# Where the stationary halves start: 64 or 192 bytes into their buffers

## The chip, the core and the metric

The kernel runs on one core of a Trainium2 chip. A core has a matrix engine (TensorE, PE in the profile, with its weight loads shown apart as PEld), a vector engine (VectorE, DVE), a scalar engine (ScalarE, ACT), GpSimd (POOL) and a queue engine (SyncE, SP) that here issues most of the transfers from the chip's memory. Data lie in an on-chip memory of 128 partitions (SBUF); a product is accumulated in a second memory (PSUM). The metric is the device time of one execution in microseconds, lower is better. The kernel before takes 1235.01 us, the median of three runs (1234.71 to 1235.12).

## The reference

A decoder trunk of two layers works on 256 tokens of width 2048, in float32. Cut to what matters:

```python
def reference(x, c, ada_w, ada_b, ln_g, ln_b, a_in_w, ..., a_out_w, kv_w, b_in_w, b_out_w):
    for layer in range(2):
        shift, scale, gate = _adaln(c, ada_w[layer], ada_b[layer])
        h = x * (1.0 + scale) + shift
        if layer < 1:
            y = _ssd_mixer(h, a_in_w[i], ..., a_out_w[i])      # h @ in_w (10304 wide), conv, scan, gate, @ out_w
        else:
            y = _dilated_mixer(h, k_sh, v_sh, b_in_w[i], b_out_w[i])   # h @ in_w (4096 wide), attention, gate, @ out_w
        x = _layer_norm(ALPHA * x + (1.0 + gate) * y, ln_g[layer], ln_b[layer])
        if layer == 0:
            k_sh, v_sh = _shared_kv(x, kv_w)                    # x @ kv_w (6144 wide)
    return x
```

Nearly all the work is in the products of 256 rows of activations with big weight matrices.

## The kernel before

**Each factor is split in two.** A weight piece of 128 partitions by 1024 columns (512 KB) is loaded into `raw` (`load_piece`, L90), ScalarE copies it, rounded, into `whi` (`split`, L100), and VectorE writes what the rounding left out into `wlo` (L102). The activations have been split likewise. A product is then high by high, high by low and low by high, in a rounded float32 type (fp32r) in which TensorE goes over its moving columns once. `raw` has six buffers, `whi` and `wlo` four each. A buffer of `whi` or `wlo` has 1088 columns, 4352 bytes in a partition, though a half needs 1024 columns; `halves_at(off)` takes the 1024 columns that begin `off` columns into the buffer. The pair `off` is given by one of two names: `SHORT` is 16 columns (64 bytes) for both halves, `LONG` is 0. In the built program the four `whi` buffers start at bytes 53504, 57856, 62208 and 66560 of a partition, those of `wlo` at 70912, 75264, 79616 and 83968, and the activations at 88320: all of these are multiples of 256.

**There are three ways to multiply.** In each, TensorE first loads 128 by 128 stationary values (LDWEIGHTS) and then streams moving columns past them (MATMUL).

- A *token-major* product (`tm_mults`, L213 to L215) holds activations in TensorE and streams 512 columns of `whi` or `wlo`, which lie at offset 0 (`LONG`). At the end of the kernel a few of these stream 256 columns.
- A *quad* (`cm_piece`, L151 to L153) holds 128 columns of `whi` or `wlo` (offset 64 bytes, `SHORT`) and streams 256 columns of the high or of the low activations: three matmuls for each 128 columns of weights and each 128 rows of the contraction.
- A *wide product* (`cm_wide`, L182 and L185) also holds weights, but streams the high and the low activations together: for each of 16 steps along the contraction, two matmuls of 512 columns with two blocks of `whi` (L182), then two of 256 columns with two blocks of `wlo` (L185). Its weights use `SHORT` too.

There are 40 wide products: 12 that make the mixer's inputs (`xs_wide`), 12 for the keys, and in the last layer 12 for the queries and four for the gate (`queries`, `z_gate`). That is 640 steps of four matmuls.

**The order is that of the code, with one piece begun ahead.** The list `upcoming` names the first piece of the next product and the offset it is to be written at; `begin_next` splits that piece while the last piece of the product before is multiplied, so that the next product finds its first halves in `ready`. `firsts` fills this list for the mixer, two more lines for the keys and the queries. The offset there and the one in `cm_wide` belong together. Behind the products, `background` takes small jobs from a list: the dot products of the modulation (L295), each with a transfer of 1 MB that SP issues, the steps of the normalization, and others.

Of the kernel before, what the change touches and what calls it, by code (L numbers as in the profile page):

```python
# [27 lines left out]
NG = 3  # L28
# [21 lines left out]
def trunk(ctx, tc, xT, x, c, par, cst, bias, lnrow, ada, wdt, win, wxs, wout, wk, wv, wbin, wbout, out):  # L50
# [28 lines left out]
    tri = cc[:, CT:CT + 128]  # L79
    ones = cc[:, CM:CM + 128]  # L80
    cons.tile([P, 32], F32, name="pad")
    SHORT, LONG = (16, 16), (0, 0)

    def rows(t, b):

# [2 lines left out]
    def load_piece(src):  # L88
        raw = wp.tile([P, 1024], F32, name="raw", bufs=6)
        nc.sync.dma_start(raw, src)  # L90
        return raw
# [5 lines left out]
    def split(raw, into=None, after=None, off=(0, 0)):  # L97

        hi, lo = into or halves_at(off)
        copied.append(S.activation(hi, raw, AF.Copy))  # L100
        with tc.issue_after(after) if after is not None else ExitStack():
            latest.append(V.tensor_tensor(lo, raw, hi.bitcast(F32), op=ALU.subtract))  # L102
        return hi.rearrange("p (k n) -> p k n", k=2), lo.rearrange("p (k n) -> p k n", k=2)

    jobs, latest, copied, pin = [], [], [], [None]
    upcoming, ready, owed = [], [], []

    def settle():

        while owed:  # L110
            with tc.issue_after(copied[-1].ins), tc.issue_after(latest[-1].ins):
                owed.pop(0)()

    def first_or(src, q, off=(0, 0)):

        return ready.pop() if ready else split(load_piece(src[q]), off=off)

    def begin_next():

        if upcoming:  # L120
            src, q, off = upcoming.pop(0)
            ready.append(split(load_piece(src[q]), off=off))

    def behind_next():

        stack = ExitStack()
        if ready:
            stack.enter_context(tc.issue_after(copied[-1].ins))
            stack.enter_context(tc.issue_after(latest[-1].ins))
        return stack  # L130

    def background(n, every=1):

        state[0] += n
        while state[0] >= every and jobs:
            state[0] -= every
            jobs.pop(0)()
# [17 lines left out]
    def acc_pair(pool=None):  # L155
        return [(pool or mm).tile([P, 2, L], F32, name="acc") for _ in range(2)]
# [11 lines left out]
    def cm_wide(src, dst, rate=(0, 1), moving=None, later=False):  # L168

        both, high = moving or (lambda kt: xp[:, kt], lambda kt: xhi[:, kt, :])  # L170
        ps = acc_pair()
        for q in range(KT // 4):
            w = first_or(src, q, SHORT)
            if q == 1:
                settle()
            if q == KT // 4 - 1:
                begin_next()
            hi, lo = (t.rearrange("p k n -> p (k n)").rearrange("p (k n) -> p k n", k=4) for t in w)
            for k in range(4):
                kt = 4 * q + k  # L180
                for n in range(2):
                    T.matmul(ps[n], hi[:, k, n * P:n * P + P], both(kt), start=kt == 0, stop=False,  # L182
                             skip_group_check=True)
                for n in range(2):
                    T.matmul(ps[n][:, 0, :], lo[:, k, n * P:n * P + P], high(kt), start=False, stop=kt == KT - 1,  # L185
                             skip_group_check=True)
            background(*rate)
        def put():
            for n in range(2):
                S.activation(dst[:, n, :], ps[n][:, 1, :], AF.Copy)  # L190
                V.tensor_tensor(dst[:, n, :], ps[n][:, 0, :], dst[:, n, :], op=ALU.add)

        if later:
            owed.append(put)
        else:
            with behind_next():
                put()
# [20 lines left out]
    def tm_pair():  # L218
        return [mm.tile([P, 512], F32, name="acc") for _ in range(2)]
# [103 lines left out]
    def drain():  # L323
        while jobs:
            jobs.pop(0)()
# [8 lines left out]
    with ExitStack() as cA:  # L334
# [15 lines left out]
        with ExitStack() as cS:  # L350
# [437 lines left out]

            def firsts(kind, g):
                if kind == "xs" and g > 1:  # L790
                    return [(wxs[2 * g - 4 + w], 0, SHORT) for w in range(2)]
                src, k0, _ = begun.get((kind, g), (None, 0, None))
                if src is None:
                    src = win[{"bc": g // 2, "xs": 4 + g, "z": 6 + g}[kind]]
                return [(src, k0 // 2, LONG if kind == "z" else SHORT)]
# [176 lines left out]
    def evict_v(hq, g, ps):  # L972
        vt[hq, g] = place(3 * hq + g if hq == 0 else 9 + g, [P, 2, 512])
        with behind_next():
            for b in range(2):
                S.activation(vt[hq, g][:, b, :], ps[b], AF.Copy)

    with ExitStack() as cL:
        pl = cL.enter_context(tc.tile_pool(name="pl", bufs=3))

        vps = [tm_pair(), tm_pair()]
        def high(i, b):
            for k in range(2):
                kt = 2 * (i // 2) + k
                for w in first_v[i]:
                    T.matmul(vps[i % 2][b], hx(kt)[:, b * P:b * P + P], w[:, k, :], start=kt == 0 and w is first_v[i][0],  # L986
                             stop=False)

        def low(i, b):
            for k in range(2):  # L990
                T.matmul(vps[i % 2][b], lx(2 * (i // 2) + k)[:, b * P:b * P + P], first_v[i][0][:, k, :], start=False,
                         stop=False)

        end, _ = x_quad(0)
        with tc.issue_after(end.ins):
            for n in range(1, 4):
                normalise(0, 512 * n, 512 * n + 512)
        for i in range(4):
            high(i, 0)
        for i in range(4):  # L1000
            if i == 2:
                _, tile4 = x_quad(1)
                for n in range(1, 4):
                    normalise(1, 512 * n, 512 * n + 512)
            low(i, 0)
        for i in range(4):
            high(i, 1)
            if i == 2:
                x_tile(4)
                x_tile(5)  # L1010
        for i in range(4):
            low(i, 1)
        for q in range(2, KT // 2):
            if q < KT // 2 - 1:
                x_tile(2 * q + 2)
                x_tile(2 * q + 3)
            for j in range(2):
                with tc.issue_after(end.ins):
                    w = split(load_piece(wv[2 * j][q]), after=tile4.ins if q == 2 else None)
                tm_mults(q, w, vps[j], hx, lx, 0, KT, range(2))  # L1020
        for g in range(2):
            evict_v(0, g, vps[g])

        R = (1, 2)
        pin[0] = latest[-1].ins
        with tc.issue_after(tile4.ins):
            state[0] = 0
            queue(pl, cols1[11:])
            jobs.append(lambda: gate_out(1))
            upcoming.extend((wk[2 * (2 * g + hq) + w], 0, SHORT) for hq in range(2) for g in range(NG) for w in range(2))  # L1030
            upcoming.extend((wv[1 + 2 * g], 0, LONG) for g in range(NG))
            evict_v(0, 2, tm_chunk(wv[4], hx, lx, rate=R))
            for hq in range(2):
                for g in range(NG):
                    kv[hq, g] = place(3 + 3 * hq + g, [P, 4, L])
                    for w in range(2):
                        cm_wide(wk[2 * (2 * g + hq) + w], kv[hq, g][:, 2 * w:2 * w + 2, :], rate=R, later=True)
            for g in range(NG):
                evict_v(1, g, tm_chunk(wv[1 + 2 * g], hx, lx, rate=R))
            drain()  # L1040
            late = latest[-1].ins

        ada_bias(1, slice(0, KT), slice(0, 2))
        for kt in range(KT):
            t = pl.tile([P, L], F32, name="htmp")
            S.activation(t, xhi[:, kt, :].bitcast(F32), AF.Identity, bias=shift(1, kt), scale=scale(1, kt))
            V.scalar_tensor_tensor(t, xlo[:, kt, :].bitcast(F32), scale(1, kt), t, op0=ALU.mult, op1=ALU.add)
            split_act(xhi[:, kt, :], xlo[:, kt, :], t)
# [29 lines left out]

    def queries(hq):
        qq = [pc2.tile([P, 4, L], F32, name=f"q{g}") for g in range(NG)]  # L1080
        upcoming.extend([(wbin[2 * (2 * g + hq) + w], 0, SHORT) for g in range(NG) for w in range(2)][1:])
        for g in range(NG):
            for w in range(2):
                cm_wide(wbin[2 * (2 * g + hq) + w], qq[g][:, 2 * w:2 * w + 2, :], rate=(1, 1),
                        later=(g, w) != (NG - 1, 1))
        return qq
# [291 lines left out]
```

## Time and profile before

| | |
|---|---|
| median of the runs | 1235.01 us (1234.71 to 1235.12) |
| the profiled execution, first to last instruction | 1233.4 us |
| TensorE busy | 1219.2 us, 99% |
| weight loads | 1048.7 us, 85% |
| VectorE busy | 1027.8 us, 83% |
| ScalarE busy | 701.2 us, 57% |
| moved from and to memory | 335.92 MB, 272 GB/s |
| granted TensorE clock | 1.000 |

The profiled execution's span is 1.6 us under the median of the runs, which also hold what lies before its first and after its last instruction. A row of the groups gives the engine, the operation, what it writes and reads, the shapes, the count, and then the busy time and the mean of one. For a matmul the mean of one runs from its start to its modelled end, and the next begins long before that; what a matmul costs in a row of many is the distance from its start to the next one's.

### The profile page before, as it was taken

How to read it: one execution, taken by the hardware profiler on the slowest of the kernel's cores; microseconds unless marked ns; L12 is line 12 of the kernel's file. 1: busy time of each engine (PE TensorE's matmuls, PEld its weight loads, DVE VectorE, ACT ScalarE, POOL GpSimd, SP SyncE). 2: the span in 40 equal slices, each digit the busy share in tenths (PEclk: the TensorE clock that was granted, in tenths of full speed). 3: DMA queues.
4: the chain of work that ended last, by engine and by line, in shares of the span. 5: the costliest groups of instructions: out<-in, count | busy, mean ns of one | idle time of the engine just before them, and what ended most of it. 6: DMA issues, size and time to landing. Idle time of an engine off the chain costs nothing.

```text
span 1233.4 us, 18854 instructions
## 1 busy us (share of the span) xinstructions
PE 1219.2 (99%) x7132; PEld 1048.7 (85%) x7132; DVE 1027.8 (83%) x1464; ACT 701.2 (57%) x1048; POOL 3.9 (0%) x8
## 2 busy tenths in 40 slices
PE   8999999999999999999999999999999999999998
PEld 7889988898888888888888788888888888888886
DVE  6999986999988989899768678888978866758776
ACT  4554477878597789764335544434445644445551
POOL 0000000000000000000000000000000000000001
PEclk9999999999999999999999999999999999999999
DMA  9999977687656556698998569989998774464673
GB/s 377 423 420 422 421 255 248 224 299 252 215 199 209 168 171 205 217 338 345 362 316 293 196 202 372 347 344 371 382 384 306 232 256 144 122 199 128 206 257 69
DMA packets 81371, 335.92 MB, mean 272 GB/s; under 512 B 9200, under 2 KB 9984, under 8 KB 68480
## 3 DMA queue, kind: packets, MB, share of 16 engines
q1 hardware_dynamic: 80352, 333.33, 75.0%
q0 software_dynamic: 576, 1.05, 0.6%
q8 instruction: 56, 0.92, 0.3%
q10 hardware_dynamic: 352, 0.34, 0.1%
q14 instruction: 35, 0.29, 0.1%
HBM read 331.45 MB, written 3.23 MB: 271 GB/s over the span
## 4 chain that ended last, share of the span: by engine, by line
PE 81%; DMA 10%; DVE 6%; ACT 2%; issue 1%; DVEq 0%; ACTq 0%; SPq 0%
PE acc L182 24%; PE acc L185 12%; PE acc L214 11%; PE acc L215 11%; PE acc L213 11%; DMA raw<-in_win 5%; DMA araw<-in_ada 3%; DVE wlo L102 2%; DVE araw L295 2%; PE py L776 1%; ACT whi L100 1%; PE acc L151 1%; PE acc L153 1%; PE acc L152 1%; PE acc L986 1%
## 5 line engine op out<-in xcount | busy, mean ns | idle before, releaser
L100 ACT ACTIVATE whi<-raw 128x1024 fp32r<-128x1024 f32 x389 | 408.5, 1058 | 358.7 <-PE acc L215 128.9
L102 DVE TENSOR_TENSOR wlo<-raw,whi 128x1024 fp32r<-128x1024 f32 x389 | 469.2, 1220 | 147.8 <-ACT whi L100 139.1
L182 PE MATMUL acc<-actT,whi 128*128 128x512 f32 x1280 | 402.7, 394 | 0.0
L185 PEld LDWEIGHTS acc<-actT,wlo 128*128 128x128 f32 x1280 | 239.6, 188 | 53.5 <-DVE wlo L102 0.5
L214 PE MATMUL acc<-wlo,actT 128*128 128x512 f32 x656 | 257.4, 392 | 2.8 <-DVE wlo L102 2.8
L185 PE MATMUL acc<-actT,wlo 128*128 128x256 f32 x1280 | 253.8, 280 | 0.0
L213 PE MATMUL acc<-whi,actT 128*128 128x512 f32 x656 | 253.5, 394 | 0.0
L295 DVE SCALAR_TENSOR_TENSOR araw<-araw,cb__72 128x2048 f32<-128x2048 f32 x95 | 217.0, 2284 | 2.9 <-DMA araw<-in_ada 2.6
L182 PEld LDWEIGHTS acc<-actT,whi 128*128 128x128 f32 x1280 | 193.9, 188 | 0.4
L215 PE MATMUL acc<-whi,actT 128*128 128x512 f32 x432 | 168.8, 391 | 0.0
L214 PEld LDWEIGHTS acc<-wlo,actT 128*128 128x128 f32 x656 | 123.2, 188 | 30.3 <-DVE wlo L102 5.1
L213 PEld LDWEIGHTS acc<-whi,actT 128*128 128x128 f32 x656 | 122.6, 188 | 24.2
L151 PE MATMUL acc<-actT,whi 128*128 128x256 f32 x372 | 103.1, 281 | 1.5 <-ACT actT L502 0.9
L153 PE MATMUL acc<-actT,wlo 128*128 128x256 f32 x372 | 101.9, 282 | 1.3 <-DVE wlo L102 1.1
L152 PE MATMUL acc<-actT,whi 128*128 128x256 f32 x372 | 103.1, 280 | 0.0
L215 PEld LDWEIGHTS acc<-whi,actT 128*128 128x128 f32 x432 | 81.1, 188 | 16.5
L215 PE MATMUL acc<-whi,ylo 128*128 128x512 f32 x224 | 87.6, 391 | 0.0
L151 PEld LDWEIGHTS acc<-actT,whi 128*128 128x128 f32 x372 | 69.6, 188 | 2.8 <-ACT actT L502 1.3
L153 PEld LDWEIGHTS acc<-actT,wlo 128*128 128x128 f32 x372 | 68.9, 188 | 2.5 <-DVE wlo L102 2.3
L152 PEld LDWEIGHTS acc<-actT,whi 128*128 128x128 f32 x372 | 70.6, 190 | 0.2
L215 PEld LDWEIGHTS acc<-whi,ylo 128*128 128x128 f32 x224 | 42.1, 188 | 8.5
L734 ACT ACTIVATE seg<-cbc,cumT 128x128 f32<-128x128 f32 x128 | 41.1, 389 | 3.5 <-PE py L776 2.1
(311 smaller groups left out, 1151.8 us busy)
## 6 DMA issues: line engine op xcount, KB each, us to landing
araw<-in_ada SPq DMA_DIRECT2D x96, 1024.0 KB, 7.2
raw<-in_win SPq DMA_DIRECT2D x109, 512.0 KB, 6.5
raw<-in_wout SPq DMA_DIRECT2D x64, 512.0 KB, 5.6
raw<-in_wbin SPq DMA_DIRECT2D x64, 512.0 KB, 3.8
raw<-in_wxs SPq DMA_DIRECT2D x48, 512.0 KB, 4.4
raw<-in_wv SPq DMA_DIRECT2D x48, 512.0 KB, 7.2
raw<-in_wk SPq DMA_DIRECT2D x48, 512.0 KB, 7.8
cbc<-cumd SPq DMA_DIRECT2D x16, 512.0 KB, 5.4
```

What stands on the lines that cost most here:

```text
L100: copied.append(S.activation(hi, raw, AF.Copy))
L102: latest.append(V.tensor_tensor(lo, raw, hi.bitcast(F32), op=ALU.subtract))
L151: T.matmul(o, hi[:, k, c_], ahi[:, kt, :], start=first, stop=False, skip_group_check=True)
L152: T.matmul(o, hi[:, k, c_], alo[:, kt, :], start=False, stop=False, skip_group_check=True)
L153: T.matmul(o, lo[:, k, c_], ahi[:, kt, :], start=False, stop=kt == k1 - 1, skip_group_check=True)
L182: T.matmul(ps[n], hi[:, k, n * P:n * P + P], both(kt), start=kt == 0, stop=False, skip_group_check=True)
L185: T.matmul(ps[n][:, 0, :], lo[:, k, n * P:n * P + P], high(kt), start=False, stop=kt == KT - 1, skip_group_check=True)
L213: T.matmul(o, h_, hi[:, k, :], start=kt == k0, stop=False, skip_group_check=part)
L214: T.matmul(o, h_, lo[:, k, :], start=False, stop=False, skip_group_check=part)
L215: end = T.matmul(o, l_, hi[:, k, :], start=False, stop=kt == k1 - 1, skip_group_check=part)
L295: return V.scalar_tensor_tensor(raw, raw, 1.0, cb_, op0=ALU.mult, op1=ALU.mult, accum_out=mod[layer][:, ct, j:j + 1])
L734: S.activation(seg[:, hh, b, :], cbc[:, hh, b, :], AF.Relu, bias=cumT[:, b, h0 + hh:h0 + hh + 1], scale=-1.0)
```

## The change

A third name, `WIDE`, 48 columns (192 bytes) for both halves, takes the place of `SHORT` wherever a piece is split for a wide product: in `cm_wide` itself and in the three lists that begin the first piece of a wide product ahead. The quads keep 64 bytes, the token-major products 0. Shapes, counts, buffers and the order of the instructions on every engine stay as they are; a half then takes bytes 192 to 4288 of its 4352. What differs is the address that ScalarE and VectorE write, and that the weight loads of the wide products read.

```diff
@@ -79,7 +79,7 @@
-    SHORT, LONG = (16, 16), (0, 0)
+    SHORT, WIDE, LONG = (16, 16), (48, 48), (0, 0)
@@ -170,7 +170,7 @@
         both, high = moving or (lambda kt: xp[:, kt], lambda kt: xhi[:, kt, :])
         ps = acc_pair()
         for q in range(KT // 4):
-            w = first_or(src, q, SHORT)
+            w = first_or(src, q, WIDE)
             if q == 1:
                 settle()
@@ -788,7 +788,7 @@
             def firsts(kind, g):
                 if kind == "xs" and g > 1:
-                    return [(wxs[2 * g - 4 + w], 0, SHORT) for w in range(2)]
+                    return [(wxs[2 * g - 4 + w], 0, WIDE) for w in range(2)]
@@ -1027,7 +1027,7 @@
-            upcoming.extend((wk[2 * (2 * g + hq) + w], 0, SHORT) for hq in range(2) for g in range(NG) for w in range(2))
+            upcoming.extend((wk[2 * (2 * g + hq) + w], 0, WIDE) for hq in range(2) for g in range(NG) for w in range(2))
@@ -1078,7 +1078,7 @@
-        upcoming.extend([(wbin[2 * (2 * g + hq) + w], 0, SHORT) for g in range(NG) for w in range(2)][1:])
+        upcoming.extend([(wbin[2 * (2 * g + hq) + w], 0, WIDE) for g in range(NG) for w in range(2)][1:])
```

## The prediction

> **What bounds the kernel now.** I read the page's busy times and its chain of waits first, to see which engine sets the end.
>
> ```profile
> PE 1219.2 (99%) x7132; PEld 1048.7 (85%) x7132; DVE 1027.8 (83%) x1464; ACT 701.2 (57%) x1048; POOL 3.9 (0%) x8
> PE 81%; DMA 10%; DVE 6%; ACT 2%; issue 1%; DVEq 0%; ACTq 0%; SPq 0%
> PE acc L182 24%; PE acc L185 12%; PE acc L214 11%; PE acc L215 11%; PE acc L213 11%; DMA raw<-in_win 5%; DMA araw<-in_ada 3%; DVE wlo L102 2%; DVE araw L295 2%; PE py L776 1%; ACT whi L100 1%; PE acc L151 1%; PE acc L153 1%; PE acc L152 1%; PE acc L986 1%
> ```
>
> TensorE is the chain: 81% of it, and the two lines of the wide products alone (L182, L185) are 36% of the span, some 444 us. A busy matrix engine may still be streaming slower than it could, so next come the groups by shape, for the counts, and then the chain in order of time inside the wide products, for what one step costs.
>
> ```profile
> L182 PE MATMUL acc<-actT,whi 128*128 128x512 f32 x1280 | 402.7, 394 | 0.0
> L185 PE MATMUL acc<-actT,wlo 128*128 128x256 f32 x1280 | 253.8, 280 | 0.0
> L182 PEld LDWEIGHTS acc<-actT,whi 128*128 128x128 f32 x1280 | 193.9, 188 | 0.4
> L185 PEld LDWEIGHTS acc<-actT,wlo 128*128 128x128 f32 x1280 | 239.6, 188 | 53.5 <-DVE wlo L102 0.5
> ```
>
> ```profile
> 256.92 0.46 PE acc L182 x2
> ...
> 278.41 0.46 PE acc L182 x2
> ```
>
> 1280 matmuls of each kind in fours make 640 steps. Each chain row above begins one step; between these two lie 31 steps in 21.49 us, so one step takes 0.6932 us, and in the sequence of the key products the rows are spaced the same. Nothing is waited for: the idle time before both MATMUL groups is 0.0.
>
> **What a matmul costs elsewhere.** The change moves only addresses, so the question is whether the address of the stationary values changes a matmul's price. The timeline shows loads and matmuls together, here in a quad (start, duration, engine):
>
> ```profile
> 211.14 0.28 PE L152 MATMUL acc<-actT,whi 128*128 128x256 f32 x1
> 211.15 0.19 PEld L153 LDWEIGHTS acc<-actT,wlo 128*128 128x128 f32 x1
> 211.26 0.28 PE L153 MATMUL acc<-actT,wlo 128*128 128x256 f32 x1
> ```
>
> The load for the next matmul starts with the matmul before it and runs beside it: two streams read the on-chip memory at once. Four pairs of timeline rows then price the same fp32r matmul in four places.
>
> ```profile
> 211.73 0.28 PE L151 MATMUL acc<-actT,whi 128*128 128x256 f32 x1
> ...
> 214.09 0.28 PE L153 MATMUL acc<-actT,wlo 128*128 128x256 f32 x1
> ```
>
> ```profile
> 250.07 0.28 PE L152 MATMUL acc<-actT,whi 128*128 128x256 f32 x1
> ...
> 251.54 0.28 PE L153 MATMUL acc<-actT,wlo 128*128 128x256 f32 x1
> ```
>
> ```profile
> 1219.58 0.28 PE L213 MATMUL acc<-whi,s 128*128 128x256 f32 x1
> ...
> 1220.90 0.28 PE L215 MATMUL acc<-whi,s 128*128 128x256 f32 x1
> ```
>
> ```profile
> 639.83 0.39 PE L213 MATMUL acc<-whi,actT 128*128 128x512 f32 x1
> ...
> 642.33 0.39 PE L215 MATMUL acc<-whi,ylo 128*128 128x512 f32 x1
> ```
>
> A quad's 256 columns (weights at 64 bytes) cost 2.36 us over 20 distances, 0.118, in the first pair, and 1.47 over 13, 0.113, in the second: same code, same addresses, two prices. At the end of the kernel 256 columns with the stationary values at offset 0 cost 1.32 over 11, 0.120. 512 columns with offset 0 cost 2.50 over 11, 0.227. Now the wide step: two of 512 and two of 256. With the dear price, 2 x 0.227 + 2 x 0.120 = 0.694, which is what it takes (0.693). With the cheap one, 2 x 0.227 + 2 x 0.113 = 0.680. So **the wide step pays today, at 64 bytes, the price that the rows show for offset 0**; the quads pay less at the same 64 bytes, and in some stretches nothing extra. No transfer and no other engine sets these prices, since the rows between each pair are spaced alike whatever runs beside them; what is left is how the load's reads fall against the moving reads.
>
> **The change part by part.** The split itself: ScalarE and VectorE write the halves 128 bytes further on.
>
> ```profile
> L100 ACT ACTIVATE whi<-raw x40: 1061/1062/1067, 580.8 to 685.6; 128x1024 fp32r<-128x1024 f32 x40
> L100 ACT ACTIVATE whi<-raw x47: 1048/1065/1069, 767.0 to 894.5; 128x1024 fp32r<-128x1024 f32 x47
> ```
>
> The first row is a stretch of token-major products (offset 0), the second the key products (offset 64): the medians are 1062 and 1065 ns, so the writer does not care, and I cost this part at nothing. If it did, by even 50 ns a piece, the cover would be the wait below: ScalarE stands idle for TensorE there.
>
> The wide step: no row has weights at 192 bytes, so I bound it. Below: the cheapest prices shown, 0.680, a saving of 0.0124 us if I take the unrounded distances (0.6932 against 2 x 0.2273 + 2 x 0.1131 = 0.6808); times 640 steps that is 7.9 us. Above: the dearest that the rows show for a wide step, which is in the first steps of the key products:
>
> ```profile
> 766.48 0.47 PE acc L182 x2
> 767.18 0.47 PE acc L182 x2
> 767.89 0.46 PE acc L182 x2
> 768.58 0.46 PE acc L182 x2
> ```
>
> 0.70, then 0.71, then 0.69: two steps in 1.41 us, 0.705 each, are 0.0118 us more than the settled 0.6932, which over 640 steps would be 7.6 us. I take the lower bound. My reason is that the wide step already sits at the dear end of every settled row: there is one dearer price, and it lasts two steps, while the cheap one holds for hundreds of matmuls in the quads once it is reached. A new phase between the two streams has more room to gain than to lose. From the 7.9 us I take 0.4 for the four products that run among the attention's small matmuls (some 8 of 16 steps each have other work between, 4 x 8 x 0.0124), since there the phase is broken each time. **Sum: -7.5 us**, 1233.4 to 1225.9 in the profiled execution, and with the 1.6 us that lie outside its span, **1227.5 us** for the median of the runs.
>
> Would the saved time reach the end? These rows are the waits and the stretches of the keys (766 to 899) and of one mixer pair:
>
> ```profile
> ACT s L190 <- PE acc L185: 34.3, 9, 4.6
> ACT whi L100 <- DMA raw<-in_wk: 10.4, 4, 3.4
> ```
>
> ```profile
> 285.00:307.30 22.30, 22.30 (x135) 19.43 (x130) 22.30 (x41) 22.14 (x43) 0.00 (x0) 1.00 0.76 266
> 766.30:899.40 133.10, 133.10 (x769) 116.73 (x768) 114.55 (x119) 56.96 (x74) 0.00 (x0) 1.00 0.94 363
> ```
>
> Among the keys ScalarE waits 34.3 us for TensorE and 10.4 for transfers, which fill 0.94 of their time there at 363 GB/s. A step 1.8% shorter asks for 370 GB/s, and the page shows slices of over 420, so they follow, without much to spare. In the mixer pair VectorE is busy 22.30 of 22.30 us; if it sets the pace there instead, the 12 mixer products (12 x 16 x 0.0124 = 2.4 us) give nothing, which the range holds.
>
> **The rivals.** *Nothing changes* (1235.0). The price follows a pattern that repeats every 64 or 128 bytes, and 192 falls on the same place as 64. For it: the wide prices are the same in all four buffers of the ring, which lie 256 bytes apart within each 1024. Against it: 64 and 0 have different rows, 0.118 and 0.120, so 64 is not a full period of the pattern; 128 may be. A rule bears on this: the Trainium skill, "SBUF — State Buffer", section "Who interferes with whom", says that TensorE has two independent read ports, one for the moving operand and one for LDWEIGHTS, and that "PE and ACT never wait on anyone"; by it the address could not matter at all and the time would be 1235.0. The pair 0.118 and 0.113 for the same quad speaks against taking it that far.
>
> *It gets slower* (1242.6). The step settles at the transient price of 0.705 instead of 0.6932: 640 x 0.0118 = 7.6 us. The place is L182 to L185 in all 640 steps; the mechanism is that a stationary row 128 bytes further on makes its reads meet the moving reads in the matmuls of 512 columns as well, which today, by their 0.227 in the token-major rows, lose nothing extra. It decides as soon as the extra for the two long matmuls exceeds the 0.0124 us that the two short ones can give back. For it: such steps exist. Against it: they give way to the settled step after two.
>
> *Half of it* (1231.2): one of the two short matmuls becomes cheap, 640 x 0.0062 = 4.0 us. I count it with the faster case. *The change doesn't do what it says*: a first piece begun ahead keeps 64 bytes; then 40 of 160 pieces would be unchanged. The three lists are changed along with the product, so I give this nothing.
>
> **How the numbers follow.** Faster 0.47 (the full sum likelier than half), unchanged 0.33, slower 0.20. A measurement of this kernel tells about 0.2%, 2.5 us, from no change, and all the priced cases lie beyond that or at zero, so the three chances are these. The predicted time is that of the likeliest, 1227.5. Its own range is 1226 to 1232.5. The range reaches from 1225.5 (the whole 7.9 us, and 1.6 more for an error of 0.0025 us in the distance of a step as read from rows of two decimals) over the unchanged case to 1239.0, a slower case of half the transient's price; left out is the full slower case and what lies beyond.
>
> **What would show it.** Right: the chain rows of L182 in the wide products stand 0.680 or 0.681 us apart instead of 0.693, the quads and token-major rows keep their distances, and ScalarE's 34.3 us of waiting for TensorE among the keys shrinks. Unchanged: 0.693 again. Slower: 0.70 or more, step after step. My sum is wrong in its second part if the rows stand at 0.680 but the time falls by less than 6 us: then VectorE in the mixer or the transfers of the keys took it back, and TensorE would show waits at L185 or L182 that are 0.0 now.

## The result and the profile after

The changed kernel takes **1232.72 us** (median of 19 runs, 1231.51 to 1234.53), the kernel before 1234.63 us beside it (19 runs, 1233.62 to 1237.40). The ratio is **0.9983**, 95% interval 0.9977 to 0.9989: 2.1 us faster, between 1.4 and 2.8. The sign of the forecast was right, its size was not: 7.5 us were forecast, and the gain lies below the 0.2% that counted as a difference.

The page of the changed kernel shows the same engine in the chain, with the same two lines of the wide products at 36% of it.

```profile
PE 1216.1 (99%) x7132; PEld 1045.7 (85%) x7132; DVE 1026.8 (83%) x1464; ACT 700.3 (57%) x1048; POOL 3.9 (0%) x8
PE 82%; DMA 7%; DVE 6%; ACT 3%; issue 2%; ACTq 0%; DVEq 0%; SPq 0%
...
L182 PE MATMUL acc<-actT,whi 128*128 128x512 f32 x1280 | 400.8, 393 | 0.0
```

The chain in order of time (start, duration, what) gives the step. First the kernel before among the keys, then the changed kernel there:

```profile
801.17 0.46 PE acc L182 x2
...
831.67 0.46 PE acc L182 x2
```

```profile
801.00 0.46 PE acc L182 x2
...
831.36 0.46 PE acc L182 x2
```

44 steps lie between the two rows of each pair: 30.50 us before, 30.36 after, so a step went from 0.6932 to **0.690 us**. The starts of single matmuls show more: before, every settled step is 0.6933; now steps of 0.6933 and of 0.6867 take turns. Among the keys the four matmuls of a step took, in the mean, 0.226 and 0.236 us (512 columns), 0.118 and 0.113 (256 columns) before, and 0.227, 0.230, 0.117 and 0.116 now: the two long ones together fell from 0.462 to 0.458, the two short ones stayed at 0.232. The forecast had every step at 0.681, by cheaper short ones.

Did the 0.0033 us a step reach the end? These rows of the chain of the changed kernel are the first wide step of the first mixer pair, the last wide step of the last gate product, and the first VectorE row of the last normalization; the kernel before has the first at 256.92 (quoted in the prediction) and the other two in the second fence.

```profile
258.34 0.46 PE acc L182 x2
...
1178.65 0.46 PE acc L182 x2
...
1228.79 0.48 DVE u L1283
```

```profile
1179.30 0.46 PE acc L182 x2
...
1229.42 0.48 DVE u L1283
```

From the first wide step to the last: 922.38 us before, 920.31 after, 2.07 us less, and 639 x 0.0033 is 2.1. From there to the end both take the same (50.12 and 50.14). But the two agree in part by chance. Added up over the starts of the matmuls, the wide products' own steps give 1.73 of the 2.07 us. The missing 0.4 lie in products that begin behind other work or are cut up by it: they take a few steps of 0.70 or more to settle, in places more than before, and one in the mixer waits longer for VectorE (see below). The other 0.36 us come mostly from a wait in a stretch of token-major products, which the change doesn't touch. TensorE's waits between 560 and 600 us in the profiled execution of the kernel before show it; the changed kernel's has none there.

```profile
PE acc L214 <- DVE wlo L102: 0.4, 1, 0.4
```

With this wait the matmul starts 0.77 us after the one before it, in the changed kernel 0.23. So the step's price gave some 1.7 us of the gain, and the match with 2.1 is closer than it should be.

The profiled execution of the changed kernel is by chance the slowest of its 19 (1234.53 us, span 1232.7, against a span of 1233.4 before). Its first wide step comes 1.4 us later, in a part that the change doesn't touch and that transfers set. In the chain, one of the first transfers of weights (`raw<-in_win`, at 18 us) takes 0.6 us longer, 11.43 us against 10.82. I didn't follow the rest of the 1.4 us. It is why the spans differ by 0.7 us only, while the medians differ by 1.9.

### The profile page after: what moved, and what is told of

Its sections match the earlier page's. It is cut to its first block, busy times and chain, and to the rows that moved or that the text cites. A ratio compares the mean times of both kernels' runs of the same rounds, so it can differ in the third digit from the quotient of the medians.

```text
span 1232.7 us, 18854 instructions
## 1 busy us (share of the span) xinstructions
PE 1216.1 (99%) x7132; PEld 1045.7 (85%) x7132; DVE 1026.8 (83%) x1464; ACT 700.3 (57%) x1048; POOL 3.9 (0%) x8
## 4 chain that ended last, share of the span: by engine, by line
PE 82%; DMA 7%; DVE 6%; ACT 3%; issue 2%; ACTq 0%; DVEq 0%; SPq 0%
PE acc L182 24%; PE acc L185 12%; PE acc L214 12%; PE acc L215 11%; PE acc L213 11%; DMA raw<-in_win 5%; DVE wlo L102 2%; DVE araw L295 2%; PE py L776 1%; ACT whi L100 1%; PE acc L151 1%; PE acc L153 1%; PE acc L152 1%; PE acc L986 1%; DMA raw<-in_wv 1%
```

## What the runs were to tell apart

After the result three readings stood against each other. One: the price of a step hangs on the addresses, but by steps of 0.0033 us, and 0.681 is a price that a wide step doesn't have at any address. Two: 0.681 exists, and 192 is only not its place. Three: the address doesn't matter, and 0.690 is a drift between runs. The later runs ask what it is in the address that counts.

### Many offsets in one kernel: five runs

`cm_wide` and the three lists take their offsets from tables, one pair of offsets for each product, so that one trace prices up to 34 pairs. The other four runs have other tables, some of them also for the mixer and the gate; the third also has `SHORT = (48, 48)`.

```diff
+    KEYS = [(0, 0), (0, 16), (0, 32), (0, 48), (16, 0), (16, 16), (16, 32), ...]
+    QUERIES = [(48, 48), (48, 0), (48, 16), (48, 32), (64, 64), (48, 48)]
-    def cm_wide(src, dst, rate=(0, 1), moving=None, later=False):
+    def cm_wide(src, dst, rate=(0, 1), moving=None, later=False, off=WIDE):
-            w = first_or(src, q, WIDE)
+            w = first_or(src, q, off)
```

> The twelve key products and the first queries each get a pair of offsets of their own (high half, low half) out of 0, 64, 128 and 192 bytes; the other wide products stay at 192. Read is the settled distance of a step of four matmuls in each product (0.6933 us at 64/64, 0.6900 at 192/192 so far). Theory A, phase: the price depends on where the loads' reads fall against the moving reads, so both halves count and the sixteen pairs show several prices between 0.680 and 0.705, 64/64 and 192/192 as before. Theory B, the low halves alone: only the loads of wlo, which run beside the long second matmul and the short first one, cost extra; pairs with the same low offset then have the same price, whatever the high one. Theory C, boundaries: a load that starts on a multiple of 256 bytes is dear or cheap by itself; the price is a sum of one number for the high and one for the low offset. 256/256 must be priced like 0/0 in all three.

> As the scan of pairs, with both halves of a product at the same offset, in steps of 16 bytes from 16 to 192 over the keys and 208, 224, 240, 8 and 4 bytes over the queries. Theory A, phase: the price changes in small steps over the 256 bytes, and is not the same for all offsets inside one 64-byte line. Theory C, boundaries in lines of 64 bytes: the offsets inside one line share its price (16, 32 and 48 like 0; 80 to 112 like 64), or every offset off a line pays for one line more.

> 34 pairs more: the 12 mixer products with the high half at 192 and the low half at the twelve multiples of 16 bytes not tried yet, the 12 key products the other way round, the queries and the gate with some others; the quads at 192 instead of 64. Phase theory: prices between 0.687 and 0.714 in steps of 0.0033 (8 cycles of 2.4 GHz), most near 0.700, few below 0.690, and the quads' settled price another than 0.118 and 0.113. If 0.680 is reached anywhere, a step can be had without any extra; if nothing is under 0.690 in 34 pairs, 192/192 is near the floor.

> Equal offsets of both halves in single columns (4 bytes) around 192, 64, 224, 0 and some others, one for each wide product. So far 63 pairs lay between 0.690 and 0.7136. If the price is fixed by the distance alone and 192 is a low point of a smooth curve: 188 and 196 lie near 0.690 to 0.693. If it jumps with every column, as 0, 4, 8 (0.6966, 0.6933, 0.7000) suggest: neighbours of 192 differ by 0.007 or more, and a distance under 0.690 may lie anywhere.

> The equal offsets in single columns that are left, and 28 bytes for one half with others for the other. By the distances so far, about one in forty is under 0.690: of 30 new ones none or one. 0.680 is expected nowhere.

Three stretches of the chain, two of the first scan (64/0, then 0/0) and one of the fourth (28/28):

```profile
812.41 0.47 PE acc L184 x2
...
820.25 0.47 PE acc L184 x2
```

```profile
767.73 0.47 PE acc L184 x2
...
775.39 0.46 PE acc L184 x2
```

```profile
891.94 0.45 PE acc L186 x2
...
900.18 0.45 PE acc L186 x2
```

11 steps in 7.84 us are 0.713, 11 in 7.66 are 0.696, 12 in 8.24 are 0.6867. Inside a product the spacing settles after a few steps. The first scan's table, in us for one settled step (from the starts of the matmuls in the trace):

| whi at byte | wlo at 0 | 64 | 128 | 192 |
|---|---|---|---|---|
| 0 | 0.697 | 0.700 | 0.700 | 0.693 |
| 64 | **0.713** | 0.693 | 0.700 | 0.693 |
| 128 | 0.707 | 0.707 | 0.697 | 0.705 |
| 192 | 0.700 or 0.707 | 0.703 | 0.703 or 0.700 | **0.690** |

256/256 cost 0.697, as 0/0 does. In the finer scans the price jumps at every 4 bytes without a plain order: 56/56 costs 0.697, 60/60 is 0.733, 64/64 is 0.693, 68/68 is 0.707, 72/72 is 0.700. The chain of the fourth scan at 60/60, where no engine is waited for:

```profile
428.30 0.50 PE acc L186 x2
...
435.63 0.50 PE acc L186 x2
```

Ten steps in 7.33 us: four bytes below 64/64, a step costs 0.040 us more. Over the five runs 126 pairs of offsets were tried, most of them in one product; 124 held a price for six steps or more, that is, a spacing that repeats step by step or over up to six steps:

| settled step, us | below 0.688 | 0.690 | 0.693 | 0.697 | 0.700 | 0.703 | 0.707 | 0.713 | 0.716 to 0.733 |
|---|---|---|---|---|---|---|---|---|---|
| pairs of offsets | 3 | 1 | 15 | 14 | 37 | 22 | 25 | 3 | 4 |

(Each column holds the pairs within about 0.002 us; some prices are the mean of steps that take turns, as at 192/192. A pair with two prices is counted where it held longest.) The three lowest are 28/28, 28/0 and 28/12, at 0.6867; the one at 0.690 is the change's. The four dearest are 204/204 (0.716), 156/156 (0.720, and 0.693 in another product), 28/156 (0.727) and 60/60. Three things follow. The address matters, so reading three falls. Most prices, 107 of the 124, lie within 0.0006 us of a ladder with rungs 0.0033 us apart, half of what lies between the two steps of the changed kernel that take turns. And no pair gives 0.681: reading two has no case among 124. The median pair costs 0.700; **64/64 was already cheaper than 105 of the 124**.

### Is it the address itself, or the distance? Two runs

The first moves everything that lies behind the constants, weights and activations alike, 64 bytes down, against the changed kernel. The second starts from the kernel before, leaves the weights at 64 and moves the activations by 128 bytes.

```diff
-    cons.tile([P, 32], F32, name="pad")
+    cons.tile([P, 16], F32, name="pad")
```

> The changed kernel with the 128-byte pad ahead of all buffers cut to 64 bytes: every buffer, the activations' too, lies 64 bytes lower, so weights start at 128 and activations at 192 of each 256 bytes, and the distance between the two streams stays. Theory A, phase between the streams: wide step 0.690, the alternation of 0.693 and 0.687 as in the changed kernel, token-major matmuls 0.227. Theory C, the address by itself: another price, and the token-major matmuls may move too.

```diff
+    act.tile([P, 32], F32, name="shift")
     hp = act.tile(...)
```

> The kernel before, its weights at 64 bytes as ever, with a pad of 128 bytes ahead of the activations: the moving operand of the wide products and quads now starts at 128 instead of 0 of each 256 bytes, so the weights lie 64 bytes behind it, which is where 192 lies to 0. Theory A (only the distance between the two streams counts): wide steps alternate 0.693 and 0.687 like those of the changed kernel, mean 0.690, though no weight has moved. Theory C (the address of the load alone counts): they stay at 0.693 each, like the kernel before. The token-major products (moving halves at 0, stationary activations now at 128) may change too.

The chain among the keys, of the run with the shorter pad and then of the one with the shifted activations:

```profile
800.85 0.46 PE acc L182 x2
...
831.21 0.46 PE acc L182 x2
```

```profile
801.30 0.46 PE acc L182 x2
...
831.66 0.46 PE acc L182 x2
```

44 steps in 30.36 us both times: 0.690, as in the changed kernel. In the first, all addresses changed and the price didn't (1233.02 us, one run, against 1235.47 beside it). In the second no weight was moved, and the wide products got the whole of the change's gain. What counts is the **distance between the address that the weight load reads and the address that the matmul's moving columns begin at, modulo 256 bytes**: 64 - 128 is 192 there. That whole multiples of 256 drop out rests on one pair, 256/256, which costs what 0/0 does.

The second run pays elsewhere. Its token-major products now load activations that lie 128 bytes off the columns they stream (starts of single matmuls, timeline):

```profile
640.00 0.39 PE L213 MATMUL acc<-whi,actT 128*128 128x512 f32 x1
...
641.62 0.39 PE L214 MATMUL acc<-wlo,actT 128*128 128x512 f32 x1
```

Seven distances in 1.62 us are 0.231; over all of them the mean is 0.2326 against 0.2275 in the kernel before. 2172 matmuls of 512 columns (the counts in the groups) by 0.0051 are 11.1 us, less 2.1 for the wide steps, 9.0. The one run took 1242.07 us, 7.3 more than the kernel before (1234.81): the sign and most of the size.

### Does a step's price times 640 give the time? The dearest pair of the first scan

All 640 steps at 64/0, to check the sum by a larger case of the other sign:

```diff
-    SHORT, WIDE, LONG = (16, 16), (48, 48), (0, 0)
+    SHORT, WIDE, LONG = (16, 16), (16, 0), (0, 0)
```

> All wide products with the high half at 64 and the low half at 0, the dearest pair of the scan (0.7134 us a step against 0.6933 at 64/64). If the settled step's price times 640 is the whole story: 640 x 0.0201 = 12.9 us slower than the kernel before, some 1247.5. If other engines or the transfers set part of the time: less than 10 us.

```profile
801.36 0.47 PE acc L182 x2
...
831.32 0.47 PE acc L182 x2
```

42 steps in 29.96 us: 0.7133. The time is 1246.10 us (median of 4) against 1234.81, ratio 1.0089 (1.0072 to 1.0106), 8.9 to 13.1 us more; 640 x (0.7133 - 0.6932) is 12.9. In its trace the wide products' own steps, added up, are 11.6 us longer. So the arithmetic of the prediction, a step's difference times 640, comes out nearly: a tenth is lost here, a fifth (1.73 of 2.1) in the change itself. A change of the same kind as the one studied can cost over five times what that one gained (11.3 us against 2.1).

### Whose loads are late? Three runs with shorter loads

At 64/0 the step costs 0.020 us more than at 64/64. In these runs `wlo`'s loads, `whi`'s, or both read half of their columns; everything is left at 64/0.

```diff
-                    T.matmul(ps[n][:, 0, :], lo[:, k, n * P:n * P + P], high(kt), ...)
+                    T.matmul(ps[n][:64, 0, :], lo[:, k, n * P:n * P + 64], high(kt), ...)
```

> The dearest pair (high 64, low 0; 0.7134 us a step), with loads of wlo of 64 columns instead of 128: the low half's share is left out for every second block of 64 outputs of the wide products. The moving columns stay the same in number and address. If the extra comes from the loads' reads beside the moving ones: shorter loads meet them less, and the step falls well below 0.7134, towards 0.69. If the moving stream makes the extra by itself, or the matmul's own start does: 0.713 as before.

```diff
-                    T.matmul(ps[n], hi[:, k, n * P:n * P + P], both(kt), ...)
+                    T.matmul(ps[n] if kt == 0 else ps[n][:64], hi[:, k, n * P:n * P + (P if kt == 0 else 64)], both(kt), ...)
```

> The dearest pair again (high 64, low 0), with full loads of wlo and loads of whi of 64 columns in 15 of 16 steps (the high half's share is left out for every second block of 64 outputs there). With both loads cut the step was 0.696, with wlo's alone 0.713. If whi's loads carry the extra alone: 0.696. If it takes both: 0.713 again. In between: each load has a part.

> As the run before, and the loads of whi are cut to 64 columns too in 15 of the 16 steps: besides, the whole share of those outputs is left out there. If the loads' reads are the cause, the step comes close to the lowest it can have, 0.680 or below, if 0.227 and 0.113 also hold something of the loads; if it stays at 0.680 exactly, the moving stream has a price of its own that no offset can take away. If loads are not the cause: 0.713.

The chain among the keys with short loads of `wlo`, then of `whi`:

```profile
801.21 0.47 PE acc L182 x2
...
831.17 0.47 PE acc L182 x2
```

```profile
801.31 0.46 PE acc L182 x2
...
831.27 0.46 PE acc L182 x2
```

42 steps in 29.96 us, 0.7133, nothing changed; and 43 in the same 29.96, 0.6967. With both short it is 0.6965. The times agree: 1246.48, 1237.19 and 1235.72 us, one run each, with 1234.69 to 1234.74 beside them. So of the extra at 64/0, 0.0166 us hang on the second half of `whi`'s loads, which are read while a matmul of 512 columns, or the last one of 256 of the step before, streams, and none on the second half of `wlo`'s. A shorter load also leaves a matmul only 64 rows of output to write instead of 128, and these runs don't tell the two apart. That loads and moving reads get in each other's way fits them, and it fits the two runs that moved both or only one of the streams; how they do it is not shown.

### Does the order of the matmuls count? Two runs

First the order within a step: high 0, high 1, low 1, low 0, with tables of pairs as above. Then, on the changed kernel, high and low by turns, in one loop.

```diff
-                for n in range(2):
+                for n in (1, 0):
                     T.matmul(ps[n][:, 0, :], lo[:, k, n * P:n * P + P], ...)
```

> The order inside a wide step is high 0, high 1, low 1, low 0 instead of high 0, high 1, low 0, low 1, and the products run through all sixteen pairs of 0, 64, 128, 192 again (keys, first queries) and twelve other equal offsets (mixer). Phase theory: the loads read other blocks at the same time, 512 bytes from the old ones, a whole number of 256, so the settled price of each pair is the same as before within 0.0005 us. If prices differ, more than the distance modulo 256 bytes counts.

```diff
                 for n in range(2):
                     T.matmul(ps[n], hi[:, k, n * P:n * P + P], ...)
-                for n in range(2):
                     T.matmul(ps[n][:, 0, :], lo[:, k, n * P:n * P + P], ...)
```

> The changed kernel (192 bytes), with the four matmuls of a wide step in the order high 0, low 0, high 1, low 1 instead of high 0, high 1, low 0, low 1: the loads beside the long matmuls are then those of wlo, those beside the short matmuls those of whi. Same work. Theory A, phase: the settled price is another one, in either direction, since the phase at the start of each load changes: between 0.680 and 0.705. Theory B, the low halves' loads: since a long matmul hides a load that is late, the price falls to 0.680.

With the two low ones exchanged the same pairs cost the same within 0.0005 us (64/0 again 0.713, 64/64 0.693, 192/192 0.690); only where a pair has two prices, as 192/0 had before, it may take the other one. High and low by turns at 192/192 is dearer. Its timeline among the keys:

```profile
801.04 0.39 PE L182 MATMUL acc<-actT,whi 128*128 128x512 f32 x1
...
803.83 0.40 PE L182 MATMUL acc<-actT,whi 128*128 128x512 f32 x1
```

Eight pairs of one high and one low in 2.79 us, 0.349 each, 0.698 a step; in other products, the queries and the gate among them, it is 0.707. One run took 1239.32 us against 1235.47. So a price doesn't belong to an offset alone: which lengths follow each other is part of it, and which of two blocks is loaded is not.

### The price of 512 columns by distance

In the token-major products the activations are the load and the weight halves the moving columns. Tables give these halves 15 offsets, and the quads lie at 128.

```diff
-    SHORT, WIDE, LONG = (16, 16), (48, 48), (0, 0)
+    SHORT, WIDE, LONG = (32, 32), (48, 48), (0, 0)
-            w = first_or(src, q)
+            w = first_or(src, q, off)
```

> The changed kernel with the moving halves of the token-major products at other offsets, one for each product: 16 to 112 bytes for the gate's, 128, 144 and 160 for three of the output's, 176 to 224 for the values'; the quads at 128. Phase theory: the long matmuls, settled at 0.2267 with offset 0, cost more at most other offsets (0.2325 at a distance of 128 in the run with moved activations), and 0 is among the lowest; if some offset is lower than 0.2267, it would be worth more than the change studied here, since there are 2280 such matmuls.

```profile
629.78 0.40 PE L216 MATMUL acc<-whi,actT 128*128 128x512 f32 x1
...
632.13 0.39 PE L217 MATMUL acc<-wlo,actT 128*128 128x512 f32 x1
```

Ten matmuls in 2.35 us: 0.235, where the kernel before has 0.227. The means by the offset of the moving halves: 0 bytes 0.2275, 112 bytes 0.2282, 64 bytes 0.2292, and the other twelve between 0.231 (16, 80, 176) and 0.2345 (208). Here the moving columns have moved and not the load, so that an offset of 64 is the distance 192, and 192 (0.2333) the distance 64. Distance 0, which these products already have, is the cheapest. The quads at 128 cost 0.1194 in the mean, against 0.1167 at 64. The kernel took 1240.18 us.

### Is there a better place? Two runs

28 bytes is the one equal offset below 0.690. First all wide products at 28; then 28 only where it had settled low, 192 elsewhere.

```diff
-    SHORT, WIDE, LONG = (16, 16), (48, 48), (0, 0)
+    SHORT, WIDE, LONG = (16, 16), (7, 7), (0, 0)
```

> The changed kernel with both halves of all wide products at 28 bytes, whose step of 0.6867 us was the lowest in the scans. If the settled step times 640 gives the time: 640 x (0.6933 - 0.6867) = 4.2 us under the kernel before, 1230.5, and 2.1 us under the changed one. If 28 was low only where that one product stood (one key product): between 1230.5 and the time of the kernel before.

```diff
+    B28 = (7, 7)
-                    cm_wide(wxs[2 * g - 4 + w], t, rate=R, ...)
+                    cm_wide(wxs[2 * g - 4 + w], t, rate=R, ..., off=B28 if g % 2 else WIDE)
...
-            cm_wide(wbin[2 * (6 + hq) + w], z, rate=(1, 2))
+            cm_wide(wbin[2 * (6 + hq) + w], z, rate=(1, 2), off=B28)
```

> 28 bytes for the 28 wide products that settled at 0.6867 with it (six mixer products, the keys, the later queries, the gate), 192 for the 12 that settled at 0.700 with 28. If a settled price hangs on the distance and on the state in which a product is entered, and both repeat: steps of 0.6867 and 0.690 in the same places, 28 x 16 x 0.0067 + 12 x 16 x 0.0033 = 3.6 us under the kernel before, 1231.0, a little under both 28 alone and 192 alone. If the state depends on what ran long before: some of the 28 products fall back to 0.700.

The first run's chain, in the keys and in the first queries:

```profile
800.80 0.45 PE acc L182 x2
...
831.70 0.45 PE acc L182 x2
```

```profile
977.96 0.47 PE acc L182 x2
...
1008.76 0.47 PE acc L182 x2
```

45 steps in 30.90 us, 0.6867; 44 in 30.80, 0.700. **The same offsets can have two prices in one kernel**: 0.6867 in 28 of the 40 products (two of them, cut up by the attention, show other spacings too), 0.700 in the other 12. By that, 28 x 16 x 0.0066 less 12 x 16 x 0.0067 is a gain of 1.7 us; measured are 1231.90 us (11 runs) against 1234.54, ratio 0.998 (0.9971 to 0.9989). The mixed kernel takes 1232.48 us (11 runs) against 1234.52, ratio 0.9981 (0.9972 to 0.9990). In its profile the keys held the low price, but the gate, which had it in the run before, didn't:

```profile
1156.36 0.47 PE acc L183 x2
...
1174.73 0.47 PE acc L183 x2
```

26 steps in 18.37 us are 0.7065, where the run before had 0.687: a third price for 28/28. Neither kernel can be told from the change itself, whose interval is 0.9977 to 0.9989. No version found beats the changed kernel by an amount that can be measured.

## Why the prediction was wrong, step by step

**What bounds the kernel** held: TensorE is the chain, the wide products 36% of it, and their MATMULs wait for nothing (0.0 before and after).

**The writers at nothing** held. ScalarE's and VectorE's busy times are 700.3 and 1026.8 us, within 1.0 of those before.

**The mechanism** held in its main part: how the load's reads fall against the moving reads sets the price, and no transfer or other engine does. The run that moved only the activations shows that the distance of the two decides. These runs don't bear out the rule of the Trainium skill that the prediction weighed ("SBUF — State Buffer", section "Who interferes with whom": two independent read ports, "PE and ACT never wait on anyone") in what it says of TensorE's two ports: the distance between what the two read moves a wide step from 0.6867 to 0.7333 us, 7%. By it the time would not have moved at all; it moved by 2.1 us here and by 11.3 at 64/0.

**The step that failed is the price of the wide step**: "I take the lower bound", -0.0124 us a step, 7.9 us, because "the wide step already sits at the dear end of every settled row". Measured were -0.0033 us a step, 2.1 us. It failed in three places.

What a step pays was misread. The prediction found that 2 x 0.227 + 2 x 0.120 is 0.694, "which is what it takes", and so held both short matmuls for dear and both long ones for free of any extra. The timeline of the kernel before says otherwise:

```profile
801.47 0.39 PE L185 MATMUL acc<-actT,wlo 128*128 128x256 f32 x2
801.70 0.62 PE L182 MATMUL acc<-actT,whi 128*128 128x512 f32 x2
802.16 0.39 PE L185 MATMUL acc<-actT,wlo 128*128 128x256 f32 x2
```

From start to start the two short ones take 0.23 us and the two long ones 0.46, where the prediction's terms are 0.240 and 0.454. One by one they are 0.226, 0.236, 0.118 and 0.113: only the sum agreed. One short matmul already had the cheap price, and most of the extra lay on the second long one. The short ones, which were to give 0.0124 us, gave nothing (0.232 together in both kernels); what was gained came from the long ones, 0.462 to 0.458.

The bound was put together from rows of other products: 0.2273 for 512 columns in the token-major ones, 0.1131 for 256 in the cheap quads. These are the cheapest prices of two other sequences at two other distances (0 and 64), one of which, the quads' 0.113, held for stretches only. At the change's distance, 192, 512 columns cost 0.2292 in the token-major products and 256 columns 0.1175 in the quads of the run with the moved activations; the same sum is then 0.693. At 64 it is 2 x 0.2333 + 2 x 0.1167 = 0.700. Measured are 0.690 and 0.693, so that even rows at the right distance miss by more than the whole effect. The sum of the prediction, 0.681, is a price that none of 124 pairs has. A step's price belongs to its sequence and its distance: high and low by turns cost 0.698 to 0.707 at the same 192/192.

And the choice between the bounds read the wrong end. The prediction had three settled prices to look at and found 0.693 the dearest. Against the 124 it is among the cheap ones: 4 are cheaper, 105 dearer. "More room to gain than to lose" was the wrong way round: there were 0.0066 us to gain and 0.040 to lose. That the change fell on the gaining side is luck as far as the prediction's reasons go. The transient 0.705, which it held against the change as the price of two steps only, is near what 25 pairs cost for good.

**The rivals.** *Nothing changes* (1235.0 against 1232.72) rested on a reason that is false: 64 and 192 aren't the same place in a shorter pattern; 64/64 and 192/192 differ, if only by one rung of 0.0033 us. *Half of it*, 1231.2, was the nearest, with the right sign at 1.5 us too much, but by a mechanism (one short matmul gets cheap) that the trace doesn't show: one was cheap before, and all steps would have been 0.687, not every second one. *Slower* was real as a mechanism, extra on the long matmuls, which one of them paid already, but for other offsets than 192.

**Would it reach the end** was answered rightly in the main: 1.73 of the 2.1 us did. VectorE in the mixer took a little back in the very pair that the prediction quoted. In its first product a load of `wlo` waits 0.30 us for VectorE, where the kernel before has 0.16, and the fifteen steps from first to last take 0.09 us more instead of 0.05 less. In the page's row of these loads the wait is 0.7 in all, against 0.5 before:

```profile
L185 PEld LDWEIGHTS acc<-actT,wlo 128*128 128x128 f32 x1280 | 239.3, 188 | 52.3 <-DVE wlo L102 0.7
```

One sign was wrong: among the keys ScalarE's wait for TensorE was to shrink from 34.3 us. The waits of the changed kernel there:

```profile
ACT s L190 <- PE acc L185: 37.4, 9, 4.6
ACT whi L100 <- DMA raw<-in_wk: 6.8, 4, 2.6
```

It grew by 3.1 us, while the wait for transfers shrank by 3.6. The two together fell by 0.5. ScalarE waits for one or for the other there, by which comes last; the split between the two is no measure of TensorE's speed.

**Left open**: why the price depends on the distance in this way, down to 4 bytes; what decides between two settled prices at the same offsets; and whether 0.2267 us for 512 columns holds an extra of its own. No run here shows it.

## What to carry to other kernels

When rows of a trace show several prices for one kind of work, ask how many settings those rows cover before calling one of them dear or cheap: here three rows were a sample out of more than a hundred prices. When a sum of such rows equals a measured total, look at the parts before naming the dear one: here the timeline of the kernel before would have shown it. A bound put together from the best rows of different sequences is an estimate that no sequence needs to reach. Where a change is one number and its price can't be derived, a kernel that gives each of its equal pieces another value of that number prices dozens of them in one trace.

## What the runs showed of the hardware

- What a row of matmuls costs depends on the distance between the address that the weight loads read and the one that the moving columns begin at. A step of 2 x 512 and 2 x 256 fp32r columns costs 0.6867 to 0.7333 us over 124 pairs of offsets, a matmul of 512 columns 0.2275 to 0.2345 over 15. Absolute addresses didn't count where they were moved (0.690 in all of the three kernels at distance 192), and 256/256 costs what 0/0 does.
- Most prices lie 0.0033 us apart or a multiple of it, and 4 bytes are enough for several such rungs: 0/0 0.697, 4/4 0.693, 8/8 0.700, but 60/60 0.733 and 64/64 0.693.
- It isn't additive in the two halves: 64/64 is 0.693 and 0/0 0.697, but 64/0 is 0.713 and 0/64 0.700.
- The same offsets can hold two prices for hundreds of matmuls: 28/28 at 0.6867 and at 0.700 in one kernel and at 0.7065 in the gate of another, the quads at 0.118 and 0.113. Which one a product takes differs between its places in the kernel, and in the gate between two kernels.
